# Recurrent loop of a hybrid encoder: a remainder's subtraction moved from GpSimd to VectorE, and three steps moved in the written order

## The chip, the core and the metric

The kernel runs on one core of a Trainium2 chip. The metric is device time in microseconds (us), the median of a few executions. Five engines have their own instruction streams: TensorE (PE in the profile, its weight loads PEld), VectorE (DVE), ScalarE (ACT), GpSimd (POOL) and SyncE (SP, which here issues the DMAs). They wait for each other through semaphores. All time stamps below are microseconds from the start of the profiled span.

## The reference, cut to what matters

The model has two layers over a sequence of 1040 tokens (16 of them prepended) and 1024 channels. The first is attention. The second, in whose loop the change lies, is this (`g` is a gain, `silu(x) = x * sigmoid(x)`):

```
z    = rms_norm(h, g)
u, gate = split(z @ w_in)                 # 2048 + 2048 channels
xc   = conv_b + sum over 4 taps of shifted(u) * conv_w[tap]
for direction in (forward, backward):     # own weights each
    r = sigmoid(blockwise(xc, w_a) + b_a) # 16 blocks of 128x128
    i = sigmoid(blockwise(xc, w_x) + b_x)
    log_a = -8 * r * softplus(-lam);  a = exp(log_a)
    b = sqrt(-expm1(2 * log_a)) * i * xc
    h_t = a_t * h_(t-1) + b_t             # scan along the tokens
y    = (h_forward + h_backward) * silu(gate)
out  = h + y @ w_out
```

## The kernel before, in words

Channels lie on the 128 partitions and tokens along the free dimension. Every float32 product is made of three matmuls: an operand is split into a rounded part (`hi`, float32r, written by a cast) and its rest (`lo`, the subtraction of `hi` from the original), and `lo*hi + hi*lo + hi*hi` are added up in PSUM. So each weight tile costs a cast (in the loop on ScalarE, L113, tile `wh`) and a subtraction on GpSimd (L116, tile `wl`; for the gate weights both tiles are called `wown`).

The second layer is a loop over 16 blocks of 128 channels, `e = 0 ... 15`, software-pipelined over three blocks: `cur` (block e, its projections, convolution and split), `prev` (block e-1, its gates, decays and first scan inputs) and `late` (block e-2, its scans, sum, gating and store). From e = 1 on PE, VectorE, ScalarE and GpSimd execute in the order in which the code is written (`manual_schedule`); SyncE's order is made by the scheduler.

In an iteration PE does: `u_mm(0)`, `u_mm(1)` (24 matmuls each, tile `pu`, 348 and 346 columns), `prev.gate(0, 0)` (tile `pz`), `u_mm(2)`, `prev.gate(1, 0)`, `g_mm(0)` (24 matmuls of 512 columns, tile `pg`), `prev.gate(0, 1)`, `g_mm(1)`, `prev.gate(1, 1)`. The tiles `pu` and `pg` take turns on three PSUM banks; a bank is free for a new tile when the last reader of the old one is done. For `u_mm(1)` that reader is `silu_out(0)` on VectorE (L1207) of the iteration before, for `u_mm(2)` it is `u_out(0)` (L1180, 348 columns) of the same iteration.

The steps that the change and the prediction speak of, with the line numbers of the kernel before:

- `root()` L1255: ScalarE, square root of a 128x2080 tile `tz`, with a load of another activation table ahead of it and behind it.
- `drive(0)`, `drive(1)` L1261: VectorE, two multiplies on `tz` with `av` (named `oa`), each with two inputs in SBUF. `mul(0)`, `mul(1)` L1241: VectorE, gate in PSUM (`pz`) times `xc`. `scan_in(d)` L1266: VectorE product of two SBUF tiles. `scan(0)`, `scan(1)` L1271, L1273; `both()` L1278; `gated()` L1282: VectorE.
- `split_xc()`: the cast `oxh` on ScalarE (L768) and the rest `oxl` on VectorE (L769) of `xc`.
- `g_in(c)` L1200: VectorE scales the gate projection in PSUM; `silu(c)` L1203: ScalarE's tanh of it; `silu_out(c)` L1207: VectorE's product `otg`.
- `store()` L1290 to L1297, only for the finished blocks 0 to 7, that is in the iterations e = 2 to 9: cast `oyh` on ScalarE, rest `oyl` on GpSimd, and two DMAs to DRAM. These are called the storing iterations below. Of the other blocks `keep()` stores the plain row.
- `w2_half(e+1, 1, 1)`: the split of the second half of the input weights for the next iteration's `u_mm`: one raw load, one cast on ScalarE, one subtraction on GpSimd.

After the loop the last two blocks are finished beside the first part of the output projection, in written order on all five engines.

Of the kernel before, what the change touches and what calls it, by code (L numbers as in the profile page):

```python
# [7 lines left out]
F32 = mybir.dt.float32  # L8
F32R = mybir.dt.float32r
# [32 lines left out]
def trunk_kernel(ctx: ExitStack, tc: tile.TileContext, a: dict, out: bass.AP):  # L42
    nc = tc.nc
# [55 lines left out]
    def split_w(src, shape, nm, own=None, eng=nc.gpsimd, own_bufs=1, raw=None):  # L99
        n = 1  # L100
        for s in shape:
            n *= s
        if raw is None:
            with tc.high_priority(sb.get("ahead", 200)):
                raw = w_raw(src, n)
        if own:
            hi, lo = [sb["P"].tile([P, 512], F32R, tag=own + z, name="wown", bufs=own_bufs) for z in "hl"]
        else:
            hi = wpool.tile([P, 512], F32R, tag="wh", name="wh", bufs=4)
            lo = wpool.tile([P, 512], F32R, tag="wl", name="wl", bufs=4)  # L110
        with tc.high_priority(sb.get("ahead", 200)):
            if sb.get("hi_act"):
                nc.scalar.copy(hi[:, :n], raw[:, :n])  # L113
            else:
                eng.tensor_scalar(hi[:, :n], raw[:, :n], 1.0, 1.0, ALU.mult, ALU.mult)  # L115
            eng.tensor_sub(lo[:, :n], raw[:, :n], hi[:, :n].bitcast(F32))  # L116
        if len(shape) == 2:
            f = lambda t: t[:, :n].rearrange("p (k m) -> p k m", k=shape[0])
        else:
            f = lambda t: t[:, :n]  # L120
        return f(hi), f(lo)
# [10 lines left out]
    def newton_rsqrt(v, shape, nm):  # L132
        y = small.tile(shape, F32, tag="nw_y" + nm, name="nw_y", bufs=1 if nm in ("72", "65", "9") else 2)
        t = small.tile(shape, F32, tag="nw_t" + nm, name="nw_t", bufs=1)
        yi = y.bitcast(I32)
        nc.vector.tensor_scalar(yi, v.bitcast(I32), 1, None, ALU.logical_shift_right)
        nc.vector.tensor_scalar(yi, yi, -1, 1597463007, ALU.mult, ALU.add)
        for _ in range(3):
            nc.vector.tensor_mul(t, y, y)
            nc.vector.scalar_tensor_tensor(t, t, -0.5, v, ALU.mult, ALU.mult)  # L140
            nc.vector.scalar_tensor_tensor(y, t, 1.5, y, ALU.add, ALU.mult)
        return y

    def flat(ap, b=65):
        return ap.rearrange("h (c b) -> (h c) b", b=b)
# [29 lines left out]
    def bank(nm, tag):  # L175
        return sb["ps"].tile([P, 512], F32, tag=tag, name=nm, bufs=sb["pcnt"][tag])
# [79 lines left out]
    for k in range(8):  # L256
        if k in (0, 1, 3, 4):
            e, hf = 3 + k % 3 % 2, k // 3
# [6 lines left out]
    for k in range(8):  # L265
        h = row("xh", "X", F32R)
        lo = row("xl", "X", F32R)
# [118 lines left out]
    for e in range(3):  # L386
        ps = run(proj1(e))
        h = row("cqh", "c", F32R)
        lo = row("cql", "c", F32R)
# [375 lines left out]
    def split(src, nm, tag, w=T, eng=nc.vector):  # L765
        hi = row(nm + "h", tag, F32R)
        lo = row(nm + "l", tag, F32R)
        nc.scalar.copy(hi[:, :w], src[:, :w])  # L768
        eng.tensor_sub(lo[:, :w], src[:, :w], hi[:, :w].bitcast(F32))  # L769
        return hi, lo  # L770
# [340 lines left out]
    def two(nm):  # L1111
        return sb["ps"].tile([P, 1024], F32, tag="two", name=nm, bufs=1)
# [33 lines left out]
    def halves(t, o=0):  # L1146
        return [(t[:, 0:512], o, o + 512), (t[:, 512:1024], o + 512, o + 1024)]

    def w2_half(e, isu, hf):
        return split_w(a["w2"][2 * e + isu, hf], (4, P), "w2")  # L1150

    def w2_load(e, isu):
        return [w2_half(e, isu, hf) for hf in range(2)]

    def chunk_mm(w, halfs, t, c0, c1):

        for hf in halfs:
            wh, wl = w[hf]
            for k in range(4):
                x, xl_ = h1h[4 * hf + k], h1l[4 * hf + k]  # L1160
                for pi, (l, r) in enumerate(((wl[:, k], x), (wh[:, k], xl_), (wh[:, k], x))):
                    nc.tensor.matmul(t[:, :c1 - c0], l, r[:, c0:c1], start=hf == 0 and k == 0 and pi == 0,  # L1162
                                     stop=hf == 1 and k == 3 and pi == 2)

    class Lru:
# [23 lines left out]
                nc.vector.scalar_tensor_tensor(xc[:, 1:T], u[:, 0:T - 1], cw[1], xc[:, 1:T], ALU.mult, ALU.add)  # L1189
                nc.vector.scalar_tensor_tensor(xc[:, 0:T - 1], u[:, 1:T], cw[3], xc[:, 0:T - 1], ALU.mult, ALU.add)  # L1190

        def split_xc(self):
            self.c = split(self.xc, "ox", "X")

        def g_in(self, c, t):

# [92 lines left out]
        def store(self):  # L1289

            e, yv = self.e, self.z[1]
            if e < 8:
                hi, lo = row("oyh", "X", F32R), row("oyl", "X", F32R)
                nc.scalar.copy(hi[:, :1024], yv[:, :1024])
                nc.gpsimd.tensor_sub(lo[:, :1024], yv[:, :1024], hi[:, :1024].bitcast(F32))
                nc.sync.dma_start(s_y[e], hi[:, :1024].bitcast(F32))
                nc.sync.dma_start(s_yl[e], lo[:, :1024].bitcast(F32))  # L1297

# [38 lines left out]
    prev = None  # L1337
    late = None
    order = ExitStack()
    w_u = w2_load(0, 1)  # L1340
    for e in range(16):
        cur = Lru(e)
        sb["hi_act"] = e > 0
        if e == 1:
            ET = mybir.EngineType
            order.enter_context(tc.manual_schedule(engines={ET.PE, ET.DVE, ET.Activation, ET.Pool}))
        if e == 0:
            w_g = w2_load(e, 0)
            raw = [bank("pu", "c") for _ in range(3)]
            chunk_mm(w_u, (0, 1), raw[0], *C3[0])  # L1350
            st_h()
            t16 = small.tile([16, 65], F32, tag="t16", name="t16", bufs=2)
            nc.sync.dma_start(t16, flat(d_vh))
            nc.vector.tensor_scalar(t16, t16, 1.0 / 1024, EPS, ALU.mult, ALU.add)
            y16 = newton_rsqrt(t16, [16, 65], "16")
            nc.sync.dma_start(flat(d_rstd2), y16)
            nc.sync.dma_start(rstd, d_rstd2.to_broadcast([P, T]))
            for c in (1, 2):
                chunk_mm(w_u, (0, 1), raw[c], *C3[c])
            w_u = w2_load(1, 1)  # L1360
            ts = halves(two("pg"), NM)
            for t, c0, c1 in ts:
                chunk_mm(w_g, (0, 1), t, c0, c1)
            cur.u = row("ou", "X")
            for c, (c0, c1) in enumerate(C3):
                nc.vector.tensor_mul(cur.u[:, c0:c1], raw[c][:, :c1 - c0], rstd[:, c0:c1])
            cur.conv()
            for c, (t, c0, c1) in enumerate(ts):
                cur.g_in(c, t)
            cur.split_xc()  # L1370
            for c in range(2):
                cur.silu(c)
                cur.silu_out(c)
            cur.weights()
            prev = cur
        else:
            w_g = w2_load(e, 0)
            cur.weights()
            if late:
                late.scan(0)  # L1380
            cur.u_mm(0, w_u)
            cur.u_out(0)
            if late:
                prev.silu_out(1)
                late.mul(1)
                late.scan_in(1)
            cur.u_mm(1, w_u)
            cur.u_out(1)
            if late:
                late.scan(1)  # L1390
                late.both()
            if e == 1:
                cur.u_mm(2, w_u)
            prev.gate(0, 0)
            prev.decay(0)
            if e > 1:
                cur.u_mm(2, w_u)
            cur.u_out(2)
            if late:
                late.gated()  # L1400
            if e < 15:
                if late:
                    late.keep()
                w_u = [w2_half(e + 1, 1, 0)]
            cur.conv()
            prev.gate(1, 0)
            prev.decay(1)
            if e < 15:
                prev.root()
                cur.g_in(0, cur.g_mm(0, w_g))  # L1410
                prev.drive(0)
                prev.drive(1)
                prev.gate(0, 1)
                w_u.append(w2_half(e + 1, 1, 1))
                cur.silu(0)
                prev.mul(0)
                prev.scan_in(0)
                cur.silu_out(0)
                cur.split_xc()
                if late:  # L1420
                    late.store()
                cur.g_in(1, cur.g_mm(1, w_g))
                cur.silu(1)
                prev.gate(1, 1)
                late, prev = prev, cur
    order.close()
    order.enter_context(tc.manual_schedule(engines={ET.PE, ET.DVE, ET.Activation, ET.Pool, ET.SP}))
# [4 lines left out]
    for e in range(4):  # L1432
        y_load(e)
    late.keep()
    cur.split_xc()
    prev.root()
    prev.drive(0)
    prev.drive(1)
# [175 lines left out]
```

## Time and profile before

| what | value |
|---|---|
| time, median of 3 runs (lowest, highest) | 1871.07 us (1869.69, 1871.14) |
| profiled execution, its own time | 1868.71 us |
| its span in the profile | 1866.9 us |
| PE busy | 1806.2 us, 97% of the span |
| DVE busy | 1218.4 us, 65% |
| ACT busy | 875.8 us, 47% |
| POOL busy | 801.2 us, 43% |
| granted clock of TensorE, mean over the span | 0.994 of full speed |

A row of the timeline gives the start, the duration, the engine, the line, the operation, and the tiles as output<-input with their sizes; "x2" is two instructions merged in one row; a bracket at the end says how long the engine was idle before the row and whom it waited for. The loop over the blocks 1 to 15 lies between about 1245 and 1680 us.

### The profile page before, as it was taken

The page shows a single profiled execution, that of the slowest core. Times are in us where ns is not written, and L with a number is a line of the kernel's source. Part 1 is how long each engine was busy: PE and PEld are TensorE (multiplying, and loading weights), DVE is VectorE, ACT ScalarE, POOL GpSimd, SP SyncE. Part 2 cuts the span into 40 slices and gives each one's busy share as a digit, 9 for nine tenths or more (in the row PEclk, how much of TensorE's full clock was granted, in tenths as well). Part 3 has the DMA queues.
Part 4 walks back from the last instruction along what each step waited for, and adds up shares of the span by engine and source line. Part 5 has one row for each costly group of instructions (what it writes and reads, how often), then busy time and mean ns, then how long its engine had stood idle before and what let it go on. Part 6 is the DMA issues. An engine that isn't in the chain of part 4 may idle for free.

```text
span 1866.9 us, 28535 instructions
## 1 busy us (share of the span) xinstructions
PE 1806.2 (97%) x10822; PEld 1646.9 (88%) x10822; DVE 1218.4 (65%) x1956; ACT 875.8 (47%) x1490; POOL 801.2 (43%) x713
## 2 busy tenths in 40 slices
PE   8999989999999999999999999999999999999999
PEld 7997888888999999888888889998888889988887
DVE  8687357787764631667777773348988989989000
ACT  5455224445442210466666662127677676674000
POOL 5446365354322463457555443332433433326331
PEclk9999999999999999999999999999999999999999
DMA  5355532223223362322222103421222222136421
GB/s 181 81 191 186 163 92 69 65 58 103 67 78 100 130 193 106 118 68 93 70 75 75 41 24 109 142 79 52 85 80 74 92 74 78 58 130 258 141 77 42
DMA packets 109333, 186.47 MB, mean 100 GB/s; under 512 B 31951, under 2 KB 51535, under 8 KB 109198
## 3 DMA queue, kind: packets, MB, share of 16 engines
q1 hardware_dynamic: 109198, 184.67, 31.1%
q8 instruction: 85, 1.39, 0.3%
q14 instruction: 50, 0.41, 0.1%
HBM read 126.72 MB, written 49.92 MB: 95 GB/s over the span
## 4 chain that ended last, share of the span: by engine, by line
PE 70%; DVE 14%; ACT 6%; POOL 5%; issue 3%; DMA 2%; SPq 0%; DVEq 0%; POOLq 0%; ACTq 0%
PE pj L168 13%; PE oo L168 10%; PE pxop L168 7%; PE pg L1162 6%; PE px L935 5%; PE pu L1162 5%; PE av L1014 4%; PE tp L998 3%; PE op L168 3%; PE up L168 3%; PE pz L128 3%; PE vps L435 2%; PE py L935 2%; DVE oxl L769 1%; DVE oz L1266 1%
## 5 line engine op out<-in xcount | busy, mean ns | idle before, releaser
L116 POOL TENSOR_TENSOR wl<-wr,wh 128x512 fp32r<-128x512 f32 (+2 forms) x218 | 321.7, 1479 | 302.1 <-ACT wh L113 269.8
L115 POOL TENSOR_SCALAR wh<-wr 128x512 fp32r<-128x512 f32 (+2 forms) x157 | 118.4, 754 | 375.0 <-PE pj L168 126.2
L168 PE MATMUL pj<-xh,wl 128*128 128x346 f32 (+1 forms) x768 | 251.3, 328 | 14.1 <-DVE wl L116 7.3
L168 PE MATMUL pj<-xl,wh 128*128 128x346 f32 (+1 forms) x768 | 248.9, 324 | 1.1 <-DVE xl L269 1.0
L168 PE MATMUL pj<-xh,wh 128*128 128x346 f32 (+1 forms) x768 | 248.3, 323 | 0.0
L168 PEld LDWEIGHTS pj<-xh,wl 128*128 128x128 f32 x768 | 146.3, 191 | 16.0 <-ACT xh L268 7.3
L168 PEld LDWEIGHTS pj<-xl,wh 128*128 128x128 f32 x768 | 146.3, 191 | 2.4 <-DVE xl L269 2.3
L168 PEld LDWEIGHTS pj<-xh,wh 128*128 128x128 f32 x768 | 146.1, 190 | 0.1
L1162 PE MATMUL pu<-h1h,wl 128*128 128x346 f32 (+1 forms) x384 | 125.2, 326 | 6.0 <-DVE ou L1180 3.0
L1162 PE MATMUL pu<-h1l,wh 128*128 128x346 f32 (+1 forms) x384 | 123.5, 321 | 0.0
L1162 PE MATMUL pu<-h1h,wh 128*128 128x346 f32 (+1 forms) x384 | 123.4, 321 | 0.0
L1004 ACT CAST pth<-tp 128x512 fp32r<-128x512 f32 (+1 forms) x160 | 79.4, 506 | 88.9 <-PE tp L998 82.6
L1005 DVE TENSOR_TENSOR ptl<-tp,pth 128x512 fp32r<-128x512 f32 (+1 forms) x160 | 92.4, 586 | 38.3 <-ACT pth L1004 37.0
L1162 PE MATMUL pg<-h1h,wl 128*128 128x512 f32 x256 | 101.4, 396 | 0.0
L168 PE MATMUL oo<-oyh,wh 128*128 128x512 f32 x256 | 101.1, 395 | 0.0
L1162 PE MATMUL pg<-h1h,wh 128*128 128x512 f32 x256 | 101.1, 395 | 0.0
L1162 PE MATMUL pg<-h1l,wh 128*128 128x512 f32 x256 | 100.8, 394 | 0.0
L168 PE MATMUL oo<-oyh,wl 128*128 128x512 f32 x256 | 100.6, 393 | 0.0
L168 PE MATMUL oo<-oyl,wh 128*128 128x512 f32 x256 | 100.4, 392 | 0.0
L998 PE MATMUL tp<-ident,p 128*128 128x128 f32 (+1 forms) x576 | 96.8, 275 | 3.6 <-POOL p L955 3.6
L1330 DVE TENSOR_TENSOR hres<-oo,hres 128x512 f32<-128x512 f32 x16 | 10.6, 688 | 129.0 <-PE oo L168 129.0
L955 POOL TENSOR_SCALAR p<-p,mmx 128x1024 f32<-128x1024 f32 (+1 forms) x72 | 83.8, 1164 | 6.4
(446 smaller groups left out, 5440.8 us busy)
## 6 DMA issues: line engine op xcount, KB each, us to landing
wr<-in_w SPq DMA_DIRECT2D x128, 256.0 KB
wr<-in_wo SPq DMA_DIRECT2D x64, 256.0 KB
s_g<-gth SPq DMA_DIRECT2D x10, 520.0 KB
xr<-in_x SPq DMA_DIRECT2D x8, 520.0 KB
s_qn<-qr SPq DMA_DIRECT2D x8, 520.0 KB
s_kn<-kr SPq DMA_DIRECT2D x8, 520.0 KB
sw<-qraw SPq DMA_DIRECT2D x16, 260.0 KB
yb<-s_yb SPq DMA_DIRECT2D x8, 520.0 KB
```

The source lines that it names most:

```text
L115: eng.tensor_scalar(hi[:, :n], raw[:, :n], 1.0, 1.0, ALU.mult, ALU.mult)
L116: eng.tensor_sub(lo[:, :n], raw[:, :n], hi[:, :n].bitcast(F32))
L128: nc.tensor.matmul(ps[:m, off + c0:off + c1], w, x[:, c0:c1], start=first and j == 0 and pi == 0, stop=last and j == nt - 1 and pi == 2)
L168: nc.tensor.matmul(t[:, :c1 - c0], w, x[:, c0:c1], start=first and j == 0 and pi == 0, stop=last and j == nt - 1 and pi == 2)
L435: nc.tensor.matmul(ps[:m, :n], s, w, start=j == 0 and pi == 0, stop=j == nt - 1 and pi == 2)
L935: nc.tensor.matmul(dst[:m, d0:d0 + a1 - a0], l[:, s], r[:, a0:a1], start=pi == 0, stop=pi == 4)
L955: nc.gpsimd.tensor_scalar(p_[:m, NM:T], p_[:m, NM:T], mx[:m, 5:6], 1.0, ALU.mult, ALU.mult)
L998: nc.tensor.transpose(tp[:, o:o + m], p_[:m, NM + P * (kt + j):NM + P * (kt + j) + P], ident[:m, :m])
L1004: nc.scalar.copy(hi[:, :w], tp[:, :w])
L1005: nc.vector.tensor_sub(lo[:, :w], tp[:, :w], hi[:, :w].bitcast(F32))
L1014: nc.tensor.matmul(av[:, :n], l[:, vs], pts[kt][o][:, j * n:j * n + n], start=kt == 0 and j == 0 and pi == 0, stop=False)
L1162: nc.tensor.matmul(t[:, :c1 - c0], l, r[:, c0:c1], start=hf == 0 and k == 0 and pi == 0, stop=hf == 1 and k == 3 and pi == 2)
```

## The change

`split_xc` is cut into `xc_hi` (ScalarE's cast) and `xc_lo` (VectorE's rest), and `g_in(1)` is now written between the two. In `store` the rest `oyl` is subtracted by VectorE and no longer by GpSimd. `silu_out(1)` goes from the next iteration, behind `u_out(0)`, to the end of the same iteration. The split `w2_half(e+1, 1, 1)` goes from behind `gate(0, 1)` to right behind `root()`.

```diff
@@ -1189,8 +1189,12 @@
                 nc.vector.scalar_tensor_tensor(xc[:, 1:T], u[:, 0:T - 1], cw[1], xc[:, 1:T], ALU.mult, ALU.add)
                 nc.vector.scalar_tensor_tensor(xc[:, 0:T - 1], u[:, 1:T], cw[3], xc[:, 0:T - 1], ALU.mult, ALU.add)
 
-        def split_xc(self):
-            self.c = split(self.xc, "ox", "X")
+        def xc_hi(self):
+            self.c = row("oxh", "X", F32R), row("oxl", "X", F32R)
+            nc.scalar.copy(self.c[0], self.xc)
+
+        def xc_lo(self):
+            nc.vector.tensor_sub(self.c[1], self.xc, self.c[0].bitcast(F32))
 
         def g_in(self, c, t):
 
@@ -1292,7 +1296,7 @@
             if e < 8:
                 hi, lo = row("oyh", "X", F32R), row("oyl", "X", F32R)
                 nc.scalar.copy(hi[:, :1024], yv[:, :1024])
-                nc.gpsimd.tensor_sub(lo[:, :1024], yv[:, :1024], hi[:, :1024].bitcast(F32))
+                nc.vector.tensor_sub(lo[:, :1024], yv[:, :1024], hi[:, :1024].bitcast(F32))
                 nc.sync.dma_start(s_y[e], hi[:, :1024].bitcast(F32))
                 nc.sync.dma_start(s_yl[e], lo[:, :1024].bitcast(F32))
 
@@ -1367,7 +1371,8 @@
             cur.conv()
             for c, (t, c0, c1) in enumerate(ts):
                 cur.g_in(c, t)
-            cur.split_xc()
+            cur.xc_hi()
+            cur.xc_lo()
             for c in range(2):
                 cur.silu(c)
                 cur.silu_out(c)
@@ -1381,7 +1386,6 @@
             cur.u_mm(0, w_u)
             cur.u_out(0)
             if late:
-                prev.silu_out(1)
                 late.mul(1)
                 late.scan_in(1)
             cur.u_mm(1, w_u)
@@ -1407,21 +1411,23 @@
             prev.decay(1)
             if e < 15:
                 prev.root()
+                w_u.append(w2_half(e + 1, 1, 1))
                 cur.g_in(0, cur.g_mm(0, w_g))
                 prev.drive(0)
                 prev.drive(1)
                 prev.gate(0, 1)
-                w_u.append(w2_half(e + 1, 1, 1))
                 cur.silu(0)
                 prev.mul(0)
                 prev.scan_in(0)
                 cur.silu_out(0)
-                cur.split_xc()
+                cur.xc_hi()
+                cur.g_in(1, cur.g_mm(1, w_g))
+                cur.xc_lo()
                 if late:
                     late.store()
-                cur.g_in(1, cur.g_mm(1, w_g))
                 cur.silu(1)
                 prev.gate(1, 1)
+                cur.silu_out(1)
                 late, prev = prev, cur
     order.close()
     order.enter_context(tc.manual_schedule(engines={ET.PE, ET.DVE, ET.Activation, ET.Pool, ET.SP}))
@@ -1432,7 +1438,8 @@
     for e in range(4):
         y_load(e)
     late.keep()
-    cur.split_xc()
+    cur.xc_hi()
+    cur.xc_lo()
     prev.root()
     prev.drive(0)
     prev.drive(1)
```

With this, `u_mm(2)` takes the bank that `silu_out(1)` frees, in place of the one that `u_out(0)` frees. PE's order and SyncE's order are the same as before.

What ScalarE has in its queue from `root()` on, in a storing iteration (`wh` is the cast of the weights, `oyh` that of the finished row), before:

```order
L1255 ACTIVATE tz<-tz 128x2080
L1237 ACT_TABLE_LOAD
L1237 ACTIVATE pz<-pz,hb 128x1040
L113 CAST wh<-wr 128x512
L1203 ACTIVATE otg<-pg 128x512
L768 CAST oxh<-oxc 128x1040
L1294 CAST oyh<-oz 128x1024
L1203 ACTIVATE otg<-pg 128x512
```

and now, the same place (the lines are those of the changed file):

```order
L1259 ACTIVATE tz<-tz 128x2080
L113 CAST wh<-wr 128x512
L1241 ACT_TABLE_LOAD
L1241 ACTIVATE pz<-pz,hb 128x1040
L1207 ACTIVATE otg<-pg 128x512
L1194 CAST oxh<-oxc 128x1040
L1298 CAST oyh<-oz 128x1024
L1207 ACTIVATE otg<-pg 128x512
```

The cast of the weights has moved ahead of the table load and of the gate's tanh.

What VectorE has in its queue from `drive(0)` on, in a storing iteration (`oxl` and `oyl` are rests, `oz<-oa,oz` is `scan(0)`), before:

```order
L1261 SCALAR_TENSOR_TENSOR tz<-oa,tz 128x1040
L1261 SCALAR_TENSOR_TENSOR tz<-oa,tz 128x1024
L1241 SCALAR_TENSOR_TENSOR oz<-pz,oxc 128x1040
L1266 TENSOR_TENSOR oz<-oz,tz 128x1040
L1207 SCALAR_TENSOR_TENSOR otg<-otg,pg 128x512
L769 TENSOR_TENSOR oxl<-oxc,oxh 128x1040
L1200 SCALAR_TENSOR_TENSOR pg<-pg,rstd 128x512
L1271 SCALAR_TENSOR_TENSOR oz<-oa,oz 128x1040
L1180 TENSOR_TENSOR ou<-pu,rstd 128x348
L1207 SCALAR_TENSOR_TENSOR otg<-otg,pg 128x512
L1241 SCALAR_TENSOR_TENSOR oz<-pz,oxc 128x1024
```

and now:

```order
L1265 SCALAR_TENSOR_TENSOR tz<-oa,tz 128x1040
L1265 SCALAR_TENSOR_TENSOR tz<-oa,tz 128x1024
L1245 SCALAR_TENSOR_TENSOR oz<-pz,oxc 128x1040
L1270 TENSOR_TENSOR oz<-oz,tz 128x1040
L1211 SCALAR_TENSOR_TENSOR otg<-otg,pg 128x512
L1204 SCALAR_TENSOR_TENSOR pg<-pg,rstd 128x512
L1197 TENSOR_TENSOR oxl<-oxc,oxh 128x1040
L1299 TENSOR_TENSOR oyl<-oz,oyh 128x1024
L1211 SCALAR_TENSOR_TENSOR otg<-otg,pg 128x512
L1275 SCALAR_TENSOR_TENSOR oz<-oa,oz 128x1040
L1180 TENSOR_TENSOR ou<-pu,rstd 128x348
L1245 SCALAR_TENSOR_TENSOR oz<-pz,oxc 128x1024
```

`pg` of the second half stands ahead of `oxl`, `oyl` is new on this engine, and the second `otg` stands ahead of the scan.

## Rows read from the trace of the kernel before

**Rows 1.** Timeline of PE: the first matmul of an iteration (`pu` of 348 columns) for the iterations e = 3, 4, 12 and 15, and the two waits within an iteration.

```profile
1301.61 0.32 PE L1162 MATMUL pu<-h1h,wl 128*128 128x348 f32 x1
1329.93 0.33 PE L1162 MATMUL pu<-h1h,wl 128*128 128x348 f32 x1
...
1361.71 0.42 PE L1162 MATMUL pu<-h1h,wl 128*128 128x348 f32 x1 [0.33 <-POOL wl L116]
...
1369.53 0.43 PE L1162 MATMUL pu<-h1h,wl 128*128 128x346 f32 x1 [0.40 <-DVE ou L1180]
...
1565.51 0.32 PE L1162 MATMUL pu<-h1h,wl 128*128 128x348 f32 x1
...
1650.52 0.32 PE L1162 MATMUL pu<-h1h,wl 128*128 128x348 f32 x1
```

**Rows 2.** Timeline of DVE from one `drive` to the next in a storing iteration.

```profile
1327.74 2.38 DVE L1261 SCALAR_TENSOR_TENSOR tz<-oa,tz 128x1040 f32<-128x1040 f32 x2 [2.30 <-ACT tz L1255]
1330.16 1.24 DVE L1241 SCALAR_TENSOR_TENSOR oz<-pz,oxc 128x1040 f32<-128x1040 f32 x1
1331.43 1.75 DVE L1266 TENSOR_TENSOR oz<-oz,tz 128x1040 f32<-128x1040 f32 x1
1333.11 0.68 DVE L1207 SCALAR_TENSOR_TENSOR otg<-otg,pg 128x512 f32<-128x512 f32 x1
1333.71 2.97 DVE L769 TENSOR_TENSOR oxl<-oxc,oxh 128x1040 fp32r<-128x1040 f32 x1
...
1337.20 2.31 DVE L1271 TENSOR_TENSOR_SCAN oz<-oa,oz 128x1040 f32<-128x1040 f32 x1
...
1341.69 1.51 DVE L1266 TENSOR_TENSOR oz<-oz,tz 128x1024 f32<-128x1024 f32 x1
...
1343.55 2.96 DVE L1273 TENSOR_TENSOR_SCAN oz<-oa,oz 128x1024 f32<-128x1024 f32 x1
1346.54 2.13 DVE L1278 TENSOR_TENSOR oz<-oz 128x1024 f32<-128x1024 f32 x1
1348.59 0.50 DVE L1180 TENSOR_TENSOR ou<-pu,rstd 128x346 f32<-128x346 f32 x1
...
1357.30 1.24 DVE L1261 SCALAR_TENSOR_TENSOR tz<-oa,tz 128x1040 f32<-128x1040 f32 x1 [2.30 <-ACT tz L1255]
```

**Rows 3.** Timeline of ACT from the end of `root()` (just ahead of the first row) at the end of the stretch of rows 2.

```profile
1357.29 1.28 ACT L1237 ACT_TABLE_LOAD   x1
1358.58 1.10 ACT L1237 ACTIVATE pz<-pz,hb 128x1040 f32<-128x1040 f32 x1
1359.61 0.61 ACT L113 CAST wh<-wr 128x512 fp32r<-128x512 f32 x1
```

**Rows 4.** Timeline of POOL in the storing iteration of rows 2.

```profile
1330.79 1.30 POOL L116 TENSOR_TENSOR wl<-wr,wh 128x512 fp32r<-128x512 f32 x1 [12.77 <-ACT wh L113]
1333.19 2.39 POOL L1295 TENSOR_TENSOR oyl<-oz,oyh 128x1024 fp32r<-128x1024 f32 x1 [1.10 <-ACT oyh L1294]
1339.57 2.55 POOL L116 TENSOR_TENSOR wl<-wr,wh 128x512 fp32r<-128x512 f32 x2 [3.98 <-PE pz L128]
1342.08 2.28 POOL L116 TENSOR_TENSOR wown<-wr,wown 128x512 fp32r<-128x512 f32 x1
...
1344.68 2.91 POOL L116 TENSOR_TENSOR wl<-wr,wh 128x512 fp32r<-128x512 f32 x1 [0.28 <-ACT wh L113]
```

**Rows 5.** Timeline of DVE in iterations without a store: two successive `drive`, the rest `oxl`, the third `ou`, and a `both` of a later iteration.

```profile
1534.64 2.38 DVE L1261 SCALAR_TENSOR_TENSOR tz<-oa,tz 128x1040 f32<-128x1040 f32 x2 [2.29 <-ACT tz L1255]
...
1540.59 1.23 DVE L769 TENSOR_TENSOR oxl<-oxc,oxh 128x1040 fp32r<-128x1040 f32 x1
...
1553.74 0.50 DVE L1180 TENSOR_TENSOR ou<-pu,rstd 128x346 f32<-128x346 f32 x1
...
1562.45 2.38 DVE L1261 SCALAR_TENSOR_TENSOR tz<-oa,tz 128x1040 f32<-128x1040 f32 x2 [2.30 <-ACT tz L1255]
...
1607.35 1.22 DVE L1278 TENSOR_TENSOR oz<-oz 128x1024 f32<-128x1024 f32 x1
```

**Rows 6.** Timelines of DVE and POOL at three other places where the two engines meet: the convolution's first tap in iteration 0 (beside a weight subtraction) and in iteration 1 (alone), and two scans after the loop beside a weight subtraction.

```profile
1246.55 2.14 DVE L1188 SCALAR_TENSOR_TENSOR oxc<-ou,vec,oxc 128x1038 f32<-128x1038 f32 x1
...
1263.49 1.30 DVE L1188 SCALAR_TENSOR_TENSOR oxc<-ou,vec,oxc 128x1038 f32<-128x1038 f32 x1 [6.32 <-ACT oxc L1187]
...
1684.33 2.73 DVE L1271 TENSOR_TENSOR_SCAN oz<-oa,oz 128x1040 f32<-128x1040 f32 x1
1684.97 3.18 POOL L116 TENSOR_TENSOR wl<-wr,wh 128x512 fp32r<-128x512 f32 x1
1686.98 3.31 DVE L1273 TENSOR_TENSOR_SCAN oz<-oa,oz 128x1024 f32<-128x1024 f32 x1
```

**Rows 7.** The last iterations and the stretch behind the loop: timeline of DVE at the `drive` of iteration 14 and at that of block 14 behind the loop, of ACT at the last gate's tanh of block 14 (`oz<-pz`, 1024 columns), and of PE in the second and third group of the following gate, which uses the same PSUM tile.

```profile
1644.12 2.38 DVE L1261 SCALAR_TENSOR_TENSOR tz<-oa,tz 128x1040 f32<-128x1040 f32 x2 [1.11 <-ACT tz L1255]
...
1673.81 2.38 DVE L1261 SCALAR_TENSOR_TENSOR tz<-oa,tz 128x1040 f32<-128x1040 f32 x2 [2.01 <-ACT tz L1255]
...
1679.23 1.11 ACT L1237 ACTIVATE oz<-pz,hb 128x1024 f32<-128x1024 f32 x1
...
1680.96 0.63 PE L128 MATMUL pz<-oxl,wown 128*128 128x512 f32 x2
1681.43 1.11 PE L128 MATMUL pz<-oxh,wown 128*128 128x512 f32 x5
```

## The prediction

> **What bounds the kernel now.** I read the engines' shares first: PE is busy for 97% of the span, so a change on VectorE, ScalarE and GpSimd can only give back what PE waits. Then PE's timeline in the loop. An iteration in which PE never waits takes 1329.93 - 1301.61 = 28.32 us [rows 1]. The eight iterations from 1329.93 to 1565.51 take 235.58 us, that is 8 x 28.32 + 9.0. These 9.0 us, 0.48% of the time, are all that the loop can give. The waits named in these iterations are one of 0.33 us for a weight's rest (`wl`, GpSimd) and one of 0.40 us for `ou` (VectorE) [rows 1].
>
> Who makes PE wait is seen on VectorE. From one `drive` to the next it takes 29.56 us [rows 2], which is the period of these iterations, and within that VectorE stands idle only for the 2.3 us ahead of `drive`, when ScalarE ends the chain from the third `ou` over convolution, tanh, exp, table load and root: from 1348.59 to 1357.30, 8.71 us [rows 2]. So VectorE (20.85 us) and ScalarE (8.71 us) form a closed ring, slower than PE; PE is dragged along, and where it waits is only where it meets the ring first. In the iterations without a store the ring takes 1562.45 - 1534.64 = 27.81 us [rows 5], less than PE, and the waits are gone. The change is worth what it does to this ring.
>
> **What an operation of VectorE costs beside GpSimd.** `oxl` takes 1.23 us alone [rows 5] and 2.97 us beside `oyl` [rows 2, 4]: GpSimd ends at 1333.19 + 2.39 = 1335.58, and `oxl` ends 1.10 us later. The same holds for `scan_in(0)` (1.75 us, ends 1.09 us after GpSimd's row), `scan(1)` (2.96 us, 2.15 us after) and `both` (2.13 us, but 1.22 us alone) [rows 2, 4, 5]; and GpSimd's subtraction at 1344.68 takes 2.91 us, ending 1.08 us after `scan(1)` [rows 2, 4]. They exclude each other for a whole instruction. `mul(0)` with one input in PSUM isn't touched: 1.24 us with GpSimd's row beginning inside it [rows 2, 4]. But a scalar_tensor_tensor with two SBUF inputs is: the convolution's tap takes 2.14 us beside GpSimd, 1.30 us alone [rows 6]. And if GpSimd waits while VectorE has two such instructions in a row, GpSimd gets in between: the subtraction issued at 1684.97 ends at 1688.15, 1.09 us after the first scan, and the second scan, whose row begins at 1686.98, ends 2.14 us later still [rows 6].
>
> The Trainium skill says the same in "SBUF — State Buffer", section "Who interferes with whom": a VectorE instruction with two SBUF inputs contends with a GpSimd instruction that reads SBUF, and whoever is second is blocked until the first is done. By that rule `drive` contends, which no row of the steady loop shows, and the sum below holds; a reader who reads the loop's rows alone, where only tensor_tensor and scans collide, would come out at the first rival. The tap's row is on the side of the rule.
>
> **The change part by part, a storing iteration.** I lay out the ring from the start of `drive` (t = 0), with the steps of rows 2.
>
> 1. The weights' cast ahead of the table load: the cast takes 0.61 us, the load 1.28, the tanh 1.10 [rows 3], so the tanh ends at 3.0 and no longer at 2.4. GpSimd's subtraction follows the beginning of the cast by 0.74 us (1359.61, and 3.05 us after `drive` in rows 4), so it is issued at 0.7, inside the first `drive`, gets in between the two, and ends at 2.3; the second `drive` ends 1.1 later, at 3.4, instead of 2.38. `mul(0)` begins at 3.36 instead of 2.42: **+0.94**. (The tanh alone would make it 3.06, +0.64.)
> 2. `scan_in(0)` no longer meets this subtraction: 1.75 to 1.23, **-0.52**.
> 3. `oxl` no longer meets `oyl`: 2.97 to 1.23, **-1.74**.
> 4. `oyl` on VectorE: bounded by 1.23 (alone) and 2.97 (beside GpSimd). GpSimd has nothing then, so 1.21 less the 0.07 by which rows overlap, **+1.14**.
> 5. `pg` and `otg` keep their cost, but `pg` is done at 7.1 instead of 9.55, so ScalarE's tanh of it, its next gate's tanh and the casts of the next weights are all earlier, and with them GpSimd's two `wl`, which begin at 11.83 before [rows 4]: now at about 9.3. That is ahead of `scan(0)` (9.9), which met nobody before. The first subtraction ends at 10.5, the scan at 12.6 (+0.44); the second runs behind it, the third (`wown`) ends at 15.0 and holds up `scan_in(1)` from 14.2 (+0.32 on the 0.28 that it loses now). The subtraction for the next first half meets `scan(1)`: 3.4 instead of 2.96 (+0.46). `both` then is free, 1.22 instead of 2.13 (-0.91); in the other order of these two the sum is the same. Together **+0.31**.
>
> Sum: +0.94 - 0.52 - 1.74 + 1.14 + 0.31 = +0.13: the ring takes 29.69. The collisions of steps 1 and 5 are not in the trace; without any (the tanh's +0.64 in step 1, and the 1.87 that `scan_in(1)`, `scan(1)` and `both` lose now given back) the ring would be 27.2 us, below PE; with all five subtractions blocking in full (1.1 each) 32.7. I take what the layout gives.
>
> **Where PE then waits.** Both named waits lose their cause: the weight's rest is ready 2 us earlier, and `u_mm(2)` waits for the second `otg` (t = 10.0) and not for the first `ou`. But `u_mm(1)` needs the bank that the first `otg` frees. That row ended at 1333.79 and the ring has no slack to give: it is at 6.5 now, 6.05 before [rows 2], and PE, not held up ahead of it any more, gets there first. So PE waits 29.69 - 28.32 = 1.37 us per iteration there, eight times: 11.0 instead of 9.0, **+2.0 us**.
>
> **Iterations without a store.** Steps 1 and 2 are +0.42. `scan(0)` now comes first (t = 8.75 to 11.1) and GpSimd's three subtractions and the fourth behind it; `scan_in(1)` ends at 14.5 and `scan(1)` at 17.75; `both` meets the fourth and ends at 19.9; the third `ou` begins at 19.86 instead of 19.10 [rows 5]. The ring takes 27.81 + 0.76 = 28.57, 0.25 above PE, in three iterations: **+0.8 us**.
>
> **Behind the loop.** Before, the ring gains on PE in these iterations; PE's iteration 15 starts 6.40 us after the last `drive` in the loop, and the following `drive` comes 23.29 us after that start [rows 1, 7]. Now PE is tied to the ring and starts about 2.65 us after `drive` (6.5 less the 3.85 us of `u_mm(0)`), and the next `drive` follows after some 28.7 (28.57, plus a cast of 1.06 that stands in that chain now, less the 0.91 of `both`), so 26.05 after PE's start: 2.8 us later. There is no room for it: the gate whose groups stand at 1680.96 and 1681.43 (0.47 apart) began at 1680.49, 0.15 us after the tanh that frees its PSUM tile (1679.23 + 1.11 = 1680.34) [rows 7]. **+2.8 us**; if all of it found room, 0.
>
> SyncE's order is the same. The store of `oyl` is issued some 1.5 us later; behind it on SyncE stand loads into tiles that GpSimd frees at t = 11 or later, so nobody waits for it.
>
> Sum: 2.0 + 0.8 + 2.8 = 5.6 us. The profiled execution takes 1868.71 and would take 1874.3; the median shown is 2.36 above it, so I add to the median: 1871.07 + 5.6 = **1876.7 us**.
>
> **The rivals.**
>
> *GpSimd doesn't get in between the two `drive`* (same). For it: no such pair met GpSimd in the loop. Against it: the two scans of rows 6. Then the subtraction waits until 2.4, `mul(0)` starts at 3.06, and the ring takes 29.39 and 28.27. The loop costs 8 x 1.07 = 8.6 (-0.4), the others nothing, the end 2.5 (0.3 less): 1873.2.
>
> *The ring falls below PE* (faster). If the weights' subtractions lie in VectorE's gaps (PSUM operations, idle 2.3 us), the ring loses all collisions and PE's waits vanish, since their named causes do: -9.0, 1862.1. It decides if the ring sheds 1.24 us. Against it: from t = 9 to 21 four of them, 1.3 us each, would have to miss 5.8 us of scans and SBUF products; three of them don't miss them now [rows 2, 4].
>
> *More collisions* (slower still). If `scan(1)` and `both` each meet a subtraction, the ring is 0.6 longer in eight iterations: +4.8, 1881.5. For it: this happens before.
>
> **How the numbers follow.** The forecast has 0.53, the first rival 0.23, the second 0.09, the third 0.15. About 0.2%, 3.7 us, is what can be told from no change: 1867.3 to 1874.8. The forecast's own range, 1874 to 1879, reaches into it slightly, so slower has 0.49 + 0.15 + 0.02 = 0.66, same 0.04 + 0.21 = 0.25, faster 0.09. The range that leaves out the second rival and the far end of the third is 1870 to 1882.
>
> **What would show it.** Right: periods of about 29.7 us in iterations 4 to 11; PE waiting at the first `pu` of 346 columns for `otg` (L1211); a `drive` row of two instructions that takes 3.4 us; `oxl` at 1.23; `scan(0)` lengthened; a wait at a `pz` behind the loop. Wrong: `drive` still 2.38 us (first rival), or a period below 28.5 us in the storing iterations.

## The result, and the profile after

The changed kernel takes 1878.1 us (median of 6 runs, 1875.99 to 1882.47), the kernel before 1869.93 us in runs beside it: a ratio of 1.0045, 95% interval [1.0035, 1.0055]. It is 8.2 us slower. Forecast were +5.6 us and 1876.7 us.

The engines' shares and the chain that ended last, from the page of the kernel after:

```profile
PE 1805.4 (96%) x10822; PEld 1645.7 (88%) x10822; DVE 1226.1 (65%) x1964; ACT 876.5 (47%) x1490; POOL 799.8 (43%) x705
...
PE 59%; DVE 22%; ACT 9%; POOL 5%; issue 3%; DMA 1%; SPq 0%; DVEq 0%; ACTq 0%; POOLq 0%
```

PE's own work is the same as before. VectorE's share of the chain that ended last has grown from 14% (on the page of before) to 22%, ScalarE's from 6% to 9%. Before, this chain runs over PE from iteration 11 on; now it stays on the ring up to the wait behind the loop.

Timeline of PE after, answering to [rows 1, 7]: the first matmuls of the iterations 4, 12 and 15, the wait of iteration 5, and the gates behind the loop.

```profile
1329.15 0.33 PE L1162 MATMUL pu<-h1h,wl 128*128 128x348 f32 x1
...
1364.02 0.43 PE L1162 MATMUL pu<-h1h,wl 128*128 128x346 f32 x1 [1.18 <-DVE otg L1211]
...
1567.05 0.32 PE L1162 MATMUL pu<-h1h,wl 128*128 128x348 f32 x1
...
1652.95 0.32 PE L1162 MATMUL pu<-h1h,wl 128*128 128x348 f32 x1
...
1682.12 0.72 PE L128 MATMUL pz<-oxh,wown 128*128 128x272 f32 x3 [0.44 <-ACT oz L1241]
...
1686.15 1.22 PE L128 MATMUL pz<-oxh,wown 128*128 128x512 f32 x2 [2.37 <-ACT oz L1241]
1687.17 1.05 PE L128 MATMUL pz<-oxl,wown 128*128 128x512 f32 x2
1688.02 1.74 PE L128 MATMUL pz<-oxh,wown 128*128 128x512 f32 x5
1689.60 0.64 PE L128 MATMUL pz<-oxl,wown 128*128 128x272 f32 x3
1690.08 1.10 PE L128 MATMUL pz<-oxh,wown 128*128 128x272 f32 x5
1691.02 0.63 PE L128 MATMUL pz<-oxl,wown 128*128 128x512 f32 x2
```

The iterations 4 to 11 take 1567.05 - 1329.15 = 237.90 us (29.74 each), before 235.58: +2.3. The iterations 12 to 14 take 85.90, before 85.01: +0.9. From iteration 15 to the end of the last matmul it is 216.88, before 212.12: +4.8. With 0.2 in iteration 3 that makes the 8.2. This stretch, from iteration 3 to the last matmul, is compared in all runs below; what lies ahead of it is the same code but for the iterations 1 and 2, which take 28.3 us each in all of them, and it ended anywhere from 1300.5 to 1307.3 us.

Timeline of VectorE after, from one `drive` to the next, answering to [rows 2]:

```profile
1357.48 3.47 DVE L1265 SCALAR_TENSOR_TENSOR tz<-oa,tz 128x1040 f32<-128x1040 f32 x2 [2.29 <-ACT tz L1259]
1360.87 1.23 DVE L1245 SCALAR_TENSOR_TENSOR oz<-pz,oxc 128x1040 f32<-128x1040 f32 x1
1362.13 1.24 DVE L1270 TENSOR_TENSOR oz<-oz,tz 128x1040 f32<-128x1040 f32 x1
...
1364.49 1.23 DVE L1197 TENSOR_TENSOR oxl<-oxc,oxh 128x1040 fp32r<-128x1040 f32 x1
1365.64 1.22 DVE L1299 TENSOR_TENSOR oyl<-oz,oyh 128x1024 fp32r<-128x1024 f32 x1
1366.77 0.68 DVE L1211 SCALAR_TENSOR_TENSOR otg<-otg,pg 128x512 f32<-128x512 f32 x1
1367.37 2.97 DVE L1275 TENSOR_TENSOR_SCAN oz<-oa,oz 128x1040 f32<-128x1040 f32 x1
...
1371.91 1.85 DVE L1270 TENSOR_TENSOR oz<-oz,tz 128x1024 f32<-128x1024 f32 x1
...
1374.11 3.21 DVE L1277 TENSOR_TENSOR_SCAN oz<-oa,oz 128x1024 f32<-128x1024 f32 x1
1377.35 1.23 DVE L1282 TENSOR_TENSOR oz<-oz 128x1024 f32<-128x1024 f32 x1
...
1387.21 3.47 DVE L1265 SCALAR_TENSOR_TENSOR tz<-oa,tz 128x1040 f32<-128x1040 f32 x2 [2.30 <-ACT tz L1259]
```

Timelines of ACT and POOL after in the same stretch, answering to [rows 3, 4]:

```profile
1357.35 0.61 ACT L113 CAST wh<-wr 128x512 fp32r<-128x512 f32 x1
1357.98 1.28 ACT L1241 ACT_TABLE_LOAD   x1
1359.27 1.10 ACT L1241 ACTIVATE pz<-pz,hb 128x1040 f32<-128x1040 f32 x1
...
1358.09 1.77 POOL L116 TENSOR_TENSOR wl<-wr,wh 128x512 fp32r<-128x512 f32 x1 [12.64 <-PE pz L128]
1366.86 4.57 POOL L116 TENSOR_TENSOR wl<-wr,wh 128x512 fp32r<-128x512 f32 x2 [6.99 <-ACT wh L113]
1371.39 1.29 POOL L116 TENSOR_TENSOR wown<-wr,wown 128x512 fp32r<-128x512 f32 x1
```

GpSimd's first subtraction begins 0.61 us after `drive(0)` and ends at 1359.86, 1.09 us ahead of the end of `drive(1)` at 1360.95: it got in between the two. `scan(0)` is 2.97 us and not 2.31 as in [rows 2], beside the two `wl` that are now issued earlier.

Timelines of DVE and ACT after at the last `drive` of the loop, at the cast of block 15 behind the convolution, and at the first `drive` behind the loop, answering to [rows 7]:

```profile
1650.39 3.48 DVE L1265 SCALAR_TENSOR_TENSOR tz<-oa,tz 128x1040 f32<-128x1040 f32 x2 [2.29 <-ACT tz L1259]
...
1675.22 1.06 ACT L1194 CAST oxh<-oxc 128x1040 fp32r<-128x1040 f32 x1 [0.48 <-DVE oxc L1190]
...
1679.57 2.38 DVE L1265 SCALAR_TENSOR_TENSOR tz<-oa,tz 128x1040 f32<-128x1040 f32 x2 [2.02 <-ACT tz L1259]
```

Windows of the kernel after (start:end, length, then busy time with instructions of PE, PEld, DVE, ACT and POOL, the granted clock, DMA share, GB/s), at the loop's wait and at the wait behind the loop:

```profile
1362.00:1364.00 2.00, 0.84 (x6) 0.56 (x4) 1.97 (x4) 0.79 (x1) 0.00 (x0) 1.00 0.20 81
1364.00:1366.00 2.00, 1.98 (x12) 1.98 (x13) 2.00 (x3) 1.39 (x2) 0.00 (x0) 1.00 0.45 182
...
1684.00:1686.00 2.00, 0.00 (x0) 0.00 (x0) 2.00 (x3) 2.00 (x4) 2.00 (x2) 1.00 0.64 189
1686.00:1688.00 2.00, 1.85 (x4) 1.49 (x5) 1.97 (x4) 1.12 (x2) 2.00 (x2) 0.50 1.06 370
1688.00:1690.00 2.00, 2.00 (x9) 1.68 (x8) 2.00 (x1) 0.89 (x1) 2.00 (x3) 0.64 0.89 275
```

After the wait of 2.37 us PE runs at the lower of its two clock levels (0.50 of full speed, 1.2 GHz) for some 3.4 us. After the loop's wait of 1.18 us it does not.

### The profile page after: what moved, and what is told of

It reads as the page before. It is cut to its first block, busy times and chain, and to the rows that moved or that the text cites. A ratio compares the mean times of both kernels' runs of the same rounds, so it can differ in the third digit from the quotient of the medians.

```text
span 1874.1 us, 28521 instructions
## 1 busy us (share of the span) xinstructions
PE 1805.4 (96%) x10822; PEld 1645.7 (88%) x10822; DVE 1226.1 (65%) x1964; ACT 876.5 (47%) x1490; POOL 799.8 (43%) x705
## 4 chain that ended last, share of the span: by engine, by line
PE 59%; DVE 22%; ACT 9%; POOL 5%; issue 3%; DMA 1%; SPq 0%; DVEq 0%; ACTq 0%; POOLq 0%
PE pj L168 13%; PE oo L168 9%; PE pxop L168 7%; PE px L935 6%; PE av L1014 4%; PE tp L998 3%; PE op L168 3%; PE up L168 3%; PE vps L435 2%; DVE tz L1265 2%; DVE oz L1277 2%; DVE oz L1270 2%; DVE oz L1275 2%; PE py L935 2%; DVE oz L1245 2%
## 5 line engine op out<-in xcount | busy, mean ns | idle before, releaser
L116 POOL TENSOR_TENSOR wl<-wr,wh 128x512 fp32r<-128x512 f32 (+2 forms) x218 | 343.8, 1580 | 320.9 <-ACT wh L113 279.4
```

## The experiments

"Lead" below is how long the last `drive` of the loop comes ahead of PE's iteration 15: 1650.52 - 1644.12 = 6.40 us before [rows 1, 7], 2.56 us after. The column "against before" is the stretch from iteration 3 to the last matmul, 561.03 us before.

| kernel | iterations 4 to 11, each | 12 to 14, each | from 15 to the end | lead | against before | timed ratio, 95% interval |
|---|---|---|---|---|---|---|
| before | 29.45 | 28.34 | 212.12 | 6.40 | | |
| after | 29.74 | 28.63 | 216.88 | 2.56 | +8.2 | 1.0045 [1.0035, 1.0055] |
| rest on VectorE alone | 28.84 | 28.34 | 212.11 | 6.45 | -4.9 | 0.9976 [0.9967, 0.9985] |
| early cast alone | 29.76 | 28.34 | 216.09 | 3.06 | +7.1 | 1.0037 [1.0025, 1.0050] |
| new order alone | 29.27 | 28.34 | 215.77 | 3.26 | +2.2 | 1.0011 [1.0002, 1.0019] |
| rest and cast | 29.37 | 28.34 | 216.12 | 3.04 | +3.5 | 1.0020 [1.0011, 1.0029] |
| rest and order | 29.23 | 28.34 | 215.67 | 3.24 | +1.8 | 1.0007 [0.9998, 1.0016] |
| cast and order | 29.74 | 28.62 | 216.91 | 2.57 | +8.2 | 1.0051 [1.0037, 1.0065] |
| after, second rest behind the drives | 29.19 | 28.34 | 215.97 | 3.08 | +1.8 | 1.0011 [1.0002, 1.0020] |
| after, PE's wait filled | 29.75 | 28.64 | 215.69 | 2.57 | +7.1 | 1.0052 [1.0040, 1.0065] |
| before, rest and both weight rests on VectorE | 28.30 | 28.34 | 212.13 | 6.24 | -9.2 | 0.9955 [0.9942, 0.9967] |
| before, rest and one weight rest on VectorE | 28.30 | 28.34 | 212.13 | 6.24 | -9.2 | 0.9949 [0.9936, 0.9963] |
| after, both weight rests in the gap | 28.30 | 28.34 | 212.52 | 6.24 | -8.8 | 0.9959 [0.9945, 0.9972] |

**Cast put back (rest and order stay).**

```diff
                 prev.root()
-                w_u.append(w2_half(e + 1, 1, 1))
                 cur.g_in(0, cur.g_mm(0, w_g))
                 prev.drive(0)
                 prev.drive(1)
                 prev.gate(0, 1)
+                w_u.append(w2_half(e + 1, 1, 1))
```

> The changed kernel with the cast of the input weights' second half put back behind gate(0, 1); the two other parts stay. Theory (VectorE's instructions with two SBUF inputs and GpSimd's subtractions exclude each other whole, and the early cast puts a subtraction between the two drives): the drive row is 2.4 us again and not 3.47, scan_in(0) is back to about 1.75, the storing period falls from 29.7 to 29.1 to 29.3 us, the period without a store to 28.3 (PE's own), the wait behind the loop to well under 1 us with the clock at full there; in all 0 to 2 us faster than the kernel before. Rival (the order of the gate steps and the rest on VectorE carry the loss, the cast doesn't matter): the period stays at 29.7 and the time 7 to 8 us above before.

The loop did as the theory says: `drive` 2.38, `scan_in(0)` 1.74, 29.23 us a period. The part behind the loop was a miss: PE still waits 2.20 us there and the half clock follows. Without that the kernel would have been 1.7 us faster than before.

**Order undone (rest and cast stay).** `g_in(1)` is written behind `store` again and `silu_out(1)` in the next iteration.

> The changed kernel with the order of the second gate argument undone (g_in(1) behind the store, silu_out(1) in the next iteration); the rest on VectorE and the early cast stay. Theory: the drive row stays at 3.4 to 3.5, scan(0) meets no subtraction (2.3), the storing period is about 29.4 us, the period without a store 28.3, and u_mm(1) no longer waits for the second otg row as it does now; in all 1 to 2 us slower than before. Rival (the new order is the loss): the drive row is unchanged but the time falls 5 us or more below the kernel before.

`drive` 3.48, `scan(0)` 2.31, a period of 29.37, as expected; the wait for `otg` at `u_mm(1)` shrinks to 0.54 to 0.58 us but doesn't go. In the loop it is 0.5 us faster than before, behind it 4.0 slower, which its expectation did not have: 2.37 us of wait, and the half clock (0.54 from 1684 to 1686).

**The early cast alone.**

```diff
                 prev.root()
+                w_u.append(w2_half(e + 1, 1, 1))
                 cur.g_in(0, cur.g_mm(0, w_g))
                 prev.drive(0)
                 prev.drive(1)
                 prev.gate(0, 1)
-                w_u.append(w2_half(e + 1, 1, 1))
```

> The kernel before with the early cast alone. Theory: the drive row goes from 2.38 to about 3.4 us, the storing period from 29.56 to about 29.8, the period without a store stays at PE's 28.3; 3 to 5 us slower than before. Rival (GpSimd can't get between the two drives, the cast only delays the tanh by 0.6 us and frees scan_in(0) by 0.5): drive 2.38, the period within 0.15 of 29.56, the time within 1 us of before.

Timelines of DVE and POOL of this kernel at one `drive`:

```profile
1419.24 3.47 DVE L1261 SCALAR_TENSOR_TENSOR tz<-oa,tz 128x1040 f32<-128x1040 f32 x2 [2.29 <-ACT tz L1255]
...
1419.85 1.78 POOL L116 TENSOR_TENSOR wl<-wr,wh 128x512 fp32r<-128x512 f32 x1 [10.31 <-ACT wh L113]
```

The early cast by itself makes the pair 3.47 us, so the rival, in which GpSimd can't get in, falls. 4.0 of the 7.1 us are again behind the loop, where none had been expected.

**The rest on VectorE alone.**

```diff
-                nc.gpsimd.tensor_sub(lo[:, :1024], yv[:, :1024], hi[:, :1024].bitcast(F32))
+                nc.vector.tensor_sub(lo[:, :1024], yv[:, :1024], hi[:, :1024].bitcast(F32))
```

> The kernel before with the finished row's rest on VectorE alone. Theory: oxl falls from 2.97 to 1.23, oyl takes about 1.2, the storing period is 28.9 to 29.0 us, PE waits some 0.6 us in each of the eight iterations instead of 1.1, the stretch behind the loop is as before; 4 to 5 us faster than before. Rival (GpSimd, free earlier, only meets other VectorE instructions, so the collision moves and the 1.2 us of oyl are added): the period is 29.5 or more and the time is that of before or slower.

As the theory has it: `oxl` 1.23, `oyl` 1.21, the period 28.84, nothing changed behind the loop. Of the three parts of the change this one alone is a gain.

**The second half's rest on VectorE behind the drives (the cast stays where the change put it).** `w2_hi` is the raw load and ScalarE's cast, `w2_lo` the subtraction, on VectorE.

```diff
-                w_u.append(w2_half(e + 1, 1, 1))
+                w_t = w2_hi(e + 1, 1)
                 cur.g_in(0, cur.g_mm(0, w_g))
                 prev.drive(0)
                 prev.drive(1)
+                w_u.append(w2_lo(w_t))
```

> The changed kernel; the cast of the weights' second half stays right behind the root, but its rest is subtracted by VectorE, written behind drive(1), so GpSimd has nothing to do beside the two drives. Theory (the drives are lengthened by GpSimd's subtraction alone): the drive row is 2.38 us again though the cast still stands ahead of the gate's tanh; the tanh ends 0.6 us later, which VectorE fills with the new subtraction of 0.65 to 0.75 us; the storing period falls from 29.7 to 29.2 to 29.4 us. In all between the kernel before and 3 us above it, 5 to 8 us below the changed kernel if the wait behind the loop shrinks too. Rival (the late tanh or the table load lengthens this place): the drive row stays near 3.4 us and the period at 29.7.

Timelines of DVE and ACT of this kernel:

```profile
1417.27 2.38 DVE L1279 SCALAR_TENSOR_TENSOR tz<-oa,tz 128x1040 f32<-128x1040 f32 x2 [2.29 <-ACT tz L1273]
1419.56 0.68 DVE L1162 TENSOR_TENSOR wl<-wr,wh 128x512 fp32r<-128x512 f32 x1
1420.19 1.24 DVE L1259 SCALAR_TENSOR_TENSOR oz<-pz,oxc 128x1040 f32<-128x1040 f32 x1
...
1419.05 1.10 ACT L1255 ACTIVATE pz<-pz,hb 128x1040 f32<-128x1040 f32 x1
```

The tanh is as late as in the change (1.8 us after `drive` begins), and `drive` takes 2.38: only the subtraction on GpSimd lengthens it. `mul(0)` begins 2.92 us after `drive` in place of 3.39, though VectorE does one instruction more; the period falls by 0.55. The hope that the wait behind the loop shrinks too was wrong: 2.36 us.

**PE's wait behind the loop filled.** The first group of the output projection is written between two gates of block 15.

```diff
-    for j in range(2):
-        for d in range(2):
-            cur.gate(d, j)
+    cur.gate(0, 0)
+    acc = [pair_of("oo")]
+    o_part(0, 0, acc[0], w_o[0])
+    cur.gate(1, 0)
+    for d in range(2):
+        cur.gate(d, 1)
```

> The changed kernel with the first group of the output projection (24 matmuls, 5.6 us, the same work) written ahead of gate(1, 0) of block 15, where PE now waits 2.37 us behind the loop. The loop stays as it is: periods 29.7 and 28.6. Theory (the wait itself brings the half clock of the 3.4 us behind it, which cost 1.9 us): PE waits about 1 us for the rest of the output weights and no longer 2.37, the granted clock stays at 1.00 from 1684 to 1692, and the stretch from iteration 15 to the end falls from 216.9 to 213 to 214 us: 3 to 4 us below the changed kernel. Rival (the clock falls for another reason): 0.64 to 0.50 at the same place with the wait shortened, and only 1 to 1.5 us gained.

Windows of this kernel, columns as above:

```profile
1684.00:1686.00 2.00, 1.61 (x9) 1.29 (x9) 1.94 (x3) 1.79 (x4) 1.12 (x1) 1.00 0.90 301
1686.00:1688.00 2.00, 1.35 (x7) 1.06 (x7) 2.00 (x3) 1.84 (x3) 2.00 (x3) 1.00 0.75 294
...
1696.00:1698.00 2.00, 1.00 (x5) 0.47 (x3) 2.00 (x2) 1.68 (x2) 1.92 (x2) 1.00 0.76 280
```

The clock stays at 1.00 where the long wait is gone, which speaks for the wait as its cause at this place (one profile; see the last section). The gain was a miss: 1.2 us in the trace, none in the times. PE waits 0.65 us for the output weight's rest, and 1.13 us ahead of the next output group, which takes over the PSUM tile of the last gate; the tanh that reads it ends only then, since the gates now come later. The trace names a load of `oyh` for this second wait, but these rows had been read by the group before.

**Weight rests in VectorE's gap.** On the kernel before with the finished row's rest on VectorE: the second half (or both halves) cast ahead of the convolution, the rest subtracted where VectorE waits for the root.

```diff
                 w_u = [w2_half(e + 1, 1, 0)]
+                w_t = w2_hi(e + 1, 1)
             cur.conv()
...
                 cur.g_in(0, cur.g_mm(0, w_g))
+                w_u.append(w2_lo(w_t))
                 prev.drive(0)
                 prev.drive(1)
                 prev.gate(0, 1)
-                w_u.append(w2_half(e + 1, 1, 1))
```

> The kernel before with the finished row's rest on VectorE and, besides, both halves of the input weights cast earlier by ScalarE (ahead of the convolution) and their rests subtracted by VectorE in the gap ahead of drive, where it stands idle for 2.3 us; no early cast behind the root. Theory: scan_in(0) is 1.24, scan(1) and both lose their collisions, the ring falls below PE's 28.32, so all 9 us of waits in the storing iterations go, and as the ring leads PE at iteration 15 there is no wait behind the loop and no half clock: 8 to 10 us faster than before, 1860 to 1862. Rival (the two casts stand in ScalarE's share of the ring and delay drive by their 1.1 us): the period is 28.6 to 28.9 and the gain is no more than that of the rest alone, 4 to 5 us.

> As the run before, but only the second half's rest is subtracted by VectorE in the gap; the first half's stays on GpSimd. Theory: scan_in(0) is 1.24 and scan(1) still meets one subtraction (about 3); the ring is at or just below PE's 28.32: 7 to 10 us faster than before. Rival (casts in ScalarE's share): as there, with a delay of 0.5 us, and 4 to 6 us faster.

Timelines of DVE and, at the first matmuls of the iterations 4 and 12, of PE in the kernel with one rest moved (226.41 us for eight iterations):

```profile
1441.65 0.68 DVE L1162 TENSOR_TENSOR wl<-wr,wh 128x512 fp32r<-128x512 f32 x1
1444.04 2.38 DVE L1275 SCALAR_TENSOR_TENSOR tz<-oa,tz 128x1040 f32<-128x1040 f32 x2 [1.71 <-ACT tz L1269]
...
1472.49 2.38 DVE L1275 SCALAR_TENSOR_TENSOR tz<-oa,tz 128x1040 f32<-128x1040 f32 x2 [1.70 <-ACT tz L1269]
...
1333.53 0.33 PE L1176 MATMUL pu<-h1h,wl 128*128 128x348 f32 x1
...
1559.94 0.32 PE L1176 MATMUL pu<-h1h,wl 128*128 128x348 f32 x1
```

The subtraction costs VectorE only idle time (1.71 us are left of 2.29). The ring takes 28.45 us, 0.13 more than PE, and PE never waits: eight such iterations use up 1 us of the ring's lead, and the iterations without a store (26.40 and 27.23 us for two of them) give it back. The two versions are within each other's intervals, both about 9 us faster than the kernel before and some 17 faster than the changed one. The rival, a delay by the casts, falls: ScalarE does them where it waits for the third `ou`.

**New order alone, new order with the cast, and the gap on the changed kernel.** The first is the run with the cast put back, with `oyl` on GpSimd; the second is the changed kernel with `oyl` on GpSimd; the third has the two weight rests in the gap.

> The kernel before with the new order of the second gate argument alone; the finished row's rest stays on GpSimd, the cast behind gate(0, 1). Theory (what counts is when GpSimd's instructions and VectorE's two-input ones want the memory at the same time; with the new order GpSimd goes from oyl straight on to the next weights' rests, so oyl's place matters little): the storing period is as in the run with order and rest together, 29.1 to 29.3 us, the wait behind the loop is there (about 2.2 us with a half clock behind it); 0 to 2 us from the kernel before. Rival (the steps' prices add up: +0.31 for the order alone): the period is 29.8 to 29.9 us and the time 6 us or more above before.

> The changed kernel with the finished row's rest back on GpSimd (order and cast stay). Theory: as above oyl's place matters little with the new order, so the storing period stays at 29.6 to 29.8 us and the time is that of the changed kernel, 7 to 8 us above before. Rival (prices add: undoing -1.74 + 1.14): the period is 30.2 to 30.4 us, another 4 to 5 us slower than the changed kernel.

> The changed kernel with both halves of the input weights cast ahead of the convolution and their rests on VectorE in the gap ahead of drive, in place of the early cast; rest and new order as in the change. Theory: nothing of GpSimd meets the drives or scan(1) any more, the storing period is PE's 28.32; whether the wait behind the loop comes is told by the lead of the last drive in the loop over iteration 15: over 6 us none and 8 to 10 us faster than before, under 4 us the wait of 2.2 to 2.4 us with the half clock and 4 to 6 us faster. Rival (the new order carries a loss of its own in the loop): the period is over 28.6 us.

Both rivals in which prices add fall: with the new order the period is 29.27 and 29.23 with the row's rest on GpSimd and on VectorE, and with the cast besides 29.74 and 29.74. Timelines of DVE and POOL of order and cast with `oyl` on GpSimd:

```profile
1400.94 2.26 DVE L1197 TENSOR_TENSOR oxl<-oxc,oxh 128x1040 fp32r<-128x1040 f32 x1
1403.12 0.68 DVE L1211 SCALAR_TENSOR_TENSOR otg<-otg,pg 128x512 f32<-128x512 f32 x1
1403.72 3.06 DVE L1275 TENSOR_TENSOR_SCAN oz<-oa,oz 128x1040 f32<-128x1040 f32 x1
...
1399.29 2.81 POOL L1299 TENSOR_TENSOR oyl<-oz,oyh 128x1024 fp32r<-128x1024 f32 x1 [2.98 <-PE pu L1162]
1403.30 4.57 POOL L116 TENSOR_TENSOR wl<-wr,wh 128x512 fp32r<-128x512 f32 x2 [1.20 <-ACT wh L113]
```

`oxl` loses 1.03 us to `oyl`, about what `oyl` costs on VectorE (1.13 from its start to the next row's); from the scan on the rows lie as in the changed kernel. The third run's lead is 6.24 us and there is no wait behind the loop, as its expectation tied the two; its gain, 0.41%, is just under the 8 to 10 us expected, in the trace 8.8.

## Why the prediction was right, and where it was off

- **The storing iterations**: forecast a ring of 29.69 and +2.0 us, measured 29.74 and +2.3. The signs named for this all came: the wait at the first `pu` of 346 columns for `otg` (1.18 us, and the matmul group after it starts a little late), `drive` at 3.47 for 3.4, `oxl` at 1.23, and a lengthened `scan(0)`.
- **Step 1** (+0.94, GpSimd between the two drives) is shown by three runs: the cast alone gives 3.47, the cast put back 2.38, and the early cast with the weights' rest taken off GpSimd 2.38 too. The whole of steps 1 and 2 was forecast at +0.42; the cast costs 0.31 (alone), 0.53 (with the rest), 0.48 (with the order) and 0.50 (with both) a period. The first rival fell with it. The second falls since the ring stays above PE's 28.32, the third since `both` takes 1.23 and meets no subtraction in the storing iterations. By the rule of the Trainium skill ("SBUF — State Buffer", section "Who interferes with whom") whoever is second waits for the whole instruction of the other; the trace agrees for `drive` too: `drive(1)` ends 1.09 us after GpSimd's row.
- **Steps 3 to 5** hold as a sum and not one by one. Forecast were -0.60 for the rest and +0.31 for the order. The rest alone gives -0.61; the order on top of it +0.39; but the order alone gives -0.18 and then the rest only -0.03. That step 5 came out near its +0.31 is partly luck: `scan(0)` lost 0.66 us where 0.44 had been counted, `scan(1)` 0.25 where it was 0.46. The step's price depends on what GpSimd does in that moment otherwise.
- **The iterations without a store**: ring 28.57 and +0.8 forecast, 28.62 and +0.9 measured.
- **Behind the loop** is the term that was mis-sized: +2.8 forecast, +4.8 measured, of which 3.2 are the late `drive` and 1.6 the clock. The `drive` behind the loop comes 1679.57 - 1652.95 = 26.62 us after PE's start of iteration 15, where 26.05 had been forecast and 23.29 is the time before: 3.3 us later and not 2.8. The sum had the cast of 1.06 us in that chain, but not the 0.48 us for which the cast waits for the convolution. PE loses 3.2 us by it: waits of 0.44 and 2.37 us, 0.4 where it starts again behind them and 0.3 in iteration 15, less some 0.3 that it waited at these gates before too. What was not priced at all is the clock behind the long wait. The three groups from 1686.15 to 1689.60 take 3.45 us; at full clock a row of five (three of 272 columns, two of 512) takes 1691.02 - 1690.08 = 0.94 and three of 272 take 1690.08 - 1689.60 = 0.48, so two of 512 take 0.46 and the three groups 0.46 + 0.46 + 0.94 = 1.86: the half clock cost 1.6.
- The reason given for that wait, PE tied to the ring, is only one way to it. In the runs with the cast or the order, but not both, PE is not tied in iterations 12 to 14 (28.34), and the loss is nearly the same (3.6 to 4.0). What the loss goes with is the lead: the next `drive` comes one turn of the ring after the last one in the loop, so what the lead lacks PE has to wait for. Before, the ring takes 27.83, 26.92 and 26.92 us in its last iterations and gains 3.3 us on PE; with the cast or the order it takes 28.1 to 28.3 and gains next to nothing. All eight kernels with a lead of 2.6 to 3.3 us lose 3.6 to 4.8 there (the filled one included); all five with 6.2 or more lose nothing or 0.4. What the least sufficient lead is was not tried.

## What to carry to other kernels

Before an instruction is moved between VectorE and GpSimd, or one that GpSimd waits for is issued earlier, lay out what the other engine does with two SBUF inputs at that moment: the collision moves with it, and the prices of single moves don't add. Put small subtractions where the ring's engine is idle; together with the finished row's rest, that took the whole of PE's waits in the loop away here. When a ring is about as fast as PE, look at the lead it carries out of the loop, since the first dependent work behind the loop pays for a lead that is gone.

## What was not expected of the hardware

Behind the waits of 2.2 to 2.4 us behind the loop the granted clock falls to half, in the changed kernel and in all six others that have such a wait, at once or up to 1.5 us after PE starts again, and stays there for about 3 us of matmuls (0.50 and 0.64 in the two windows after it in the changed kernel; 0.50 and 0.65 with the new order alone). In the six kernels without such a wait it stays at 1.00 there. After the loop's waits of 1.2 us, and after 0.65 and 1.13 us in the filled version, it stays at 1.00 too. So a wait of 2.4 us cost PE about 4 here.

The length of one wait does not decide it, though. Ahead of the loop, in attention, PE waits 2.63 to 2.65 us in all 13 kernels ahead of the same matmul. In four of them (new order alone, cast and order, second rest behind the drives, PE's wait filled) the clock falls to 0.50 within 1.4 us behind it; in the other nine, the changed kernel among them, it stays at 1.00. PE's timeline and the window of the changed kernel:

```profile
844.56 0.30 PE L935 MATMUL px<-kr,qrl 128*16 128x272 f32 x1 [2.64 <-POOL kr L870]
...
844.00:846.00 2.00, 1.44 (x8) 0.78 (x9) 0.30 (x1) 0.84 (x2) 0.50 (x1) 1.00 0.66 181
```

What else decides is not shown by these runs.
